# 512-column products in the output projections and in the dilated attention's q, k, v

## The chip, the cores and the metric

The kernel runs on one core of one Trainium2 chip. The metric is device time in microseconds (us) of one execution. Before the change the median of three runs is 1854.78 us (1853.63 to 1857.01).

## The reference

512 tokens of 1024 features go through two blocks, all in float32. Block 1 mixes sparse attention (8 heads) with a state-space scan, projects with `w_o`, and runs a gated feed-forward net with a short convolution. Block 2 has a gated convolution mixer and a dilated attention with three groups of windows and dilations. Cut to what the change touches:

```python
# block 1, feed-forward
u = causal_dwconv(h @ w_up, conv_w, conv_b);  a, v = split(u, 2)
x = x + gt2 * ((silu(a) * v) @ w_down)            # 2816 -> 1024
# block 2, convolution mixer
x = x + (b_gate * conv3(c_gate * u) * silu(z)) @ conv_w_out      # 2048 -> 1024
# block 2, dilated attention: 16 heads of 64, groups (128,1), (512,4), (2048,16)
proj = h @ w_in;  qkv, z = proj[..., :9216], proj[..., 9216:]
for g in range(3):
    q = rms_norm(qkv[:, :, g, 0], q_gain[g]);  k = rms_norm(qkv[:, :, g, 1], k_gain[g])
    o[g], lse[g] = dilated_group_attention(q, k, qkv[:, :, g, 2], bias[g], *DILATED_GROUPS[g])
alpha = softmax(stack(lse));  y = sum(alpha * stack(o)) * silu(z)
x = x + y @ attn_w_out                              # 1024 -> 1024
```

## The kernel before

**Products.** Each float32 product is made of three: high·high, high·low, low·high, where a number is split into a rounded high part and the rest. `wload` (L100) brings a weight piece of 128 x 1024 numbers by a DMA on SP's queue (L109) into `raw`; ACT rounds it into `whi` (all activations are recorded at L59), DVE, or POOL at a few places, subtracts to get `wlo` (L95). `raw`, `whi` and `wlo` have three buffers each. There are two loops of matmuls. `gemm_b` (L122, matmul at L133) holds the weights still and moves 512 tokens past them, so a matmul is 512 columns wide. `gemm_a` (L138, matmul at L146) holds 128 tokens still and moves weights: before, 256 columns of weights per matmul. Two tiles of 128 tokens then share one PSUM bank of 512 columns, so that a chunk of 256 weight columns for all 512 tokens takes two banks.

**Projections back to 1024 features** go through `proj_out` (L405): four chunks of 256 columns, two banks each, then `residual` (L376) adds to x and `square_sums` (L286) prepares the next norm. It serves `w_o`, `w_down` (two halves of 11 row blocks), `conv_w_out`, and `attn_w_out`, the latter once for heads 0 to 13 (seven pairs) and once for the last pair, where `done` (L1475) adds x and writes the output. PSUM has eight banks. `divide(4, 4, "acc", "acc")` (L430) gives the feed-forward and convolution stages four accumulation banks and four others; the attention has four accumulation banks (`acc`), three (`pst`) for transposes and scores, and one (`pso`) for the output of a pair.

**The attention** (`block2_attn`, L1227) walks over eight pairs of heads. For pair p:

- `v12`, the values of groups 1 and 2, is one `gemm_a` chunk of 256 columns; ACT copies it out of PSUM (`values_out`). For even p there also is `v0` and the gate `z` of two pairs, by `gemm_b`.
- For each group g a `gemm_a` chunk of 256 columns gives q and k in two banks. ACT squares the banks, DVE sums (L1333), a chain of small DVE operations makes the inverse root (`rsqrt`), and DVE multiplies the banks by it into `qn` (L1336) in SBUF, which has one buffer of 256 columns.
- PE transposes q (L1343) and k (L1351) of `qn` into `pst` banks; ACT and DVE split them into `qh`, `ql`, `kbh`, `kbl`.
- PE makes the scores (L1365 for group 0, L1382 for groups 1 and 2: twelve matmuls into two `pst` banks). DVE adds the bias and takes the extreme of each row (L1373, L1389), ACT takes exponentials into `P0`, `P1`, `P2`.
- When all three groups are there, the weights `wg` of the groups are worked out (L1405 to L1419); those of group 0 go through DRAM because its tokens lie in another order. DVE scales `P1` and `P2` block by block (L1435, 16 operations of 128 x 128), PE transposes them (L1436) and multiplies with `v12` (L1442); the same for group 0 (L1451, L1460, L1464). L1468 multiplies with the gate, and the result is split into `yh`, `yl`.

**Order.** Every engine runs its own instructions in one fixed order, which the Tile framework's scheduler decides from a simulated timeline and the priority of the code (program order, unless `tc.high_priority()` raises it). So work of the next chunk or the next pair is put between the steps of this one; where a tile has one buffer, the next writer waits for the last reader.

Of the kernel before, what the change touches and what calls it, by code (L numbers as in the profile page):

```python
# [10 lines left out]
F32 = mybir.dt.float32  # L11
# [8 lines left out]
D = 1024  # L20
# [31 lines left out]
def build(tc, A, out, dump=None, stop=None):  # L52
# [15 lines left out]
    with ExitStack() as top:  # L68
# [31 lines left out]
        def wload(ap, k, c, gain=None, eng=None, part=None, step=None):  # L100
# [4 lines left out]
            for k0 in range(0, k, step) if part is None else [part * step]:  # L105
# [3 lines left out]
                dma(raw[:, :n], ap[:, k0 * c:k0 * c + n])  # L109
# [141 lines left out]
        def ada(which):  # L251
# [4 lines left out]
            if not half:  # L256
                asum[which] = sml.tile([128, 256], F32, name="asum", bufs=3)
# [8 lines left out]
        def gate_rows(slot, tiles):  # L266

            for h, g in enumerate(tiles):
                pb = bank(acc)
                for k in range(4):  # L270
                    c = slot * 8 + h * 4 + k
                    d = sml.tile([128, 128], F32, name="gdiag")
# [13 lines left out]
        def square_sums(tiles, c, n):  # L286

            for t in range(tiles.start, tiles.stop):
                sq = sml.tile([128, 256], BF, name="nsq")
                act(sq, x[:, t, c * 256:(c + 1) * 256], AF.Square, accum_out=xss[:, n, t, c:c + 1])  # L290
# [3 lines left out]
        def scaled(g, twice=False):  # L294
# [4 lines left out]
            if not twice:  # L299
                ss = sml.tile([128, 2], F32, name="nss")  # L300
                V.tensor_reduce(ss, xss[:, 0, tl], axis=AX.X, op=OP.add)
                rs = mean_rsqrt(ss, [128, 2], "n", 1.0 / D)
            else:
# [3 lines left out]
                V.tensor_reduce(m, xss[:, 0, tl], axis=AX.X, op=OP.add)  # L307
                V.tensor_scalar(m, m, 1.0 / D, EPS, op0=OP.mult, op1=OP.add)
                V.tensor_reduce(s2, xss[:, 1, tl], axis=AX.X, op=OP.add)
# [66 lines left out]
        def residual(ps, tiles, c, gate, last, gain=None, rs=None):  # L376

            o = x[:, tiles, c * 256:(c + 1) * 256]
            src = ps.rearrange("p (t c) -> p t c", t=2)
            if gate is None:  # L380
                V.tensor_add(o, src, o)
            else:
                t = sml.tile([128, 2, 256], F32, name="rtmp", bufs=1)
                gc = gate[c // 2][:, c % 2 * 256:c % 2 * 256 + 256]
                if rs is None:
                    V.tensor_tensor(t, src, gc[:, None, :].to_broadcast([128, 2, 256]), op=OP.mult)
                else:
                    for q in range(2):
                        k = q if rs.shape[1] == 2 else tiles.start + q
                        V.scalar_tensor_tensor(t[:, q], src[:, q], rs[:, k:k + 1], gc, op0=OP.mult, op1=OP.mult)  # L390
                (V if c == 3 and last else P).tensor_tensor(o, o, t, op=OP.add)
            if last:
                square_sums(tiles, c, 0)
                if gain is not None:
                    V.tensor_tensor(o, o, gain[:, None, c * 256:(c + 1) * 256].to_broadcast([128, 2, 256]), op=OP.mult)
                    square_sums(tiles, c, 1)
# [8 lines left out]
        def proj_out(xh, xl, wname, k0, k, gate, gains=None, done=None, last=True, gain=None, rs=None, halves=(0, 1)):  # L405

            for c in range(4):
                pb = [bank(acc) if b in halves else None for b in range(2)]
                w = wload(A[wname][c][:, k0 * 256:(k0 + k) * 256], k, 256, None if gains is None else gains[:, k0:])
                tb = [t for b, t in enumerate(token_banks(pb, natural)) if b in halves]  # L410
                if c == 3 and last:
# [4 lines left out]
                for b in halves:  # L416
                    if done is not None:
                        done(pb[b], b, c)
                        continue
                    residual(pb[b], slice(2 * b, 2 * b + 2), c, gate, last, gain, rs)  # L420
                    if c == 3 and last and b == 0 and len(halves) == 2:
# [7 lines left out]
        divide(4, 4, "acc", "acc")  # L429
# [92 lines left out]
def block1_mix(tc, nc, E):  # L522
# [669 lines left out]
    def out_s():  # L1192
        gate_rows(4, gt1)
        ry = mean_rsqrt(ssq[:, 1], [128, 4], "o", 0.25 / 512)
        proj_out(xh[:, 4:8], xl[:, 4:8], "w_o", 4, 4, gt1, gains, rs=ry, last=False)

    def out_a(b):

        rs = mean_rsqrt(ssq[:, 0, 2 * b:2 * b + 2], [128, 2], "o2", 1.0 / 512)
        proj_out(xh, xl, "w_o", 0, 4, gt1, gains, rs=rs, halves=(b,))  # L1200
# [26 lines left out]
def block2_attn(tc, nc, E):  # L1227
# [16 lines left out]
    with ExitStack() as ph:  # L1244
# [20 lines left out]
        v0 = None  # L1265
        gz = [None] * 8
        for p in range(8):

            def gate_out(pz):
                for q in range(2):  # L1270
                    gz[p + q] = pp.tile([128, S], F32, name=f"yl{p + q}")
                    act(gz[p + q], pz[q], AF.Silu)
# [337 lines left out]
```

## Time and profile before

| what | value |
|---|---|
| median of three runs | 1854.78 us (1853.63 to 1857.01) |
| the profiled execution | 1851.47 us, its span 1849.1 us |
| PE busy | 97% of the span, 12252 matmuls |
| DVE busy | 59% |
| ACT busy | 43% |
| POOL busy | 16% |
| DMA | 189.55 MB, mean 103 GB/s |

The span runs from the first to the last instruction of the trace; 2.4 us of the profiled execution lie outside it. PE is TensorE, DVE VectorE, ACT ScalarE, POOL GpSimd, SP the engine that issues DMAs. Up to about 375 us runs the mixer of block 1, then the feed-forward net to about 750 us, the convolution mixer to about 1210 us, and the dilated attention to the end; two pairs of heads take 146.7 us there (the rows of one pair recur two pairs later by that much).

### The profile page before, as it was taken

The page shows a single profiled execution, that of the slowest core. Times are in us where ns is not written, and L with a number is a line of the kernel's source. Part 1 is how long each engine was busy: PE and PEld are TensorE (multiplying, and loading weights), DVE is VectorE, ACT ScalarE, POOL GpSimd, SP SyncE. Part 2 cuts the span into 40 slices and gives each one's busy share as a digit, 9 for nine tenths or more (in the row PEclk, how much of TensorE's full clock was granted, in tenths as well). Part 3 has the DMA queues.
Part 4 walks back from the last instruction along what each step waited for, and adds up shares of the span by engine and source line. Part 5 has one row for each costly group of instructions (what it writes and reads, how often), then busy time and mean ns, then how long its engine had stood idle before and what let it go on. Part 6 is the DMA issues. An engine that isn't in the chain of part 4 may idle for free.

```text
span 1849.1 us, 31264 instructions
## 1 busy us (share of the span) xinstructions
PE 1785.7 (97%) x12252; PEld 1580.2 (85%) x12252; DVE 1090.8 (59%) x2722; ACT 798.5 (43%) x1625; POOL 292.4 (16%) x238
## 2 busy tenths in 40 slices
PE   5998999999999999899999999999999999999998
PEld 3787657888898889888898888989989999989998
DVE  8796867965535554633333333346665665765775
ACT  3532666564413433432322323335455464554552
POOL 3665202431111111500000000120000000000000
PEclk9999999999999999999999999999999999999999
DMA  8358640423232233232332323222232222322222
GB/s 336 93 150 237 210 138 12 136 83 103 86 98 102 92 87 96 70 103 93 102 92 91 103 91 103 81 93 80 81 93 70 81 92 70 93 69 81 81 65 63
DMA packets 84660, 189.55 MB, mean 103 GB/s; under 512 B 31649, under 2 KB 39073, under 8 KB 84513
## 3 DMA queue, kind: packets, MB, share of 16 engines
q1 hardware_dynamic: 84512, 187.56, 31.9%
q8 instruction: 96, 1.57, 0.4%
q14 instruction: 52, 0.42, 0.1%
HBM read 182.74 MB, written 4.78 MB: 101 GB/s over the span
## 4 chain that ended last, share of the span: by engine, by line
PE 87%; DVE 7%; DMA 2%; issue 1%; ACT 1%; POOL 1%; SPq 0%; DVEq 0%; POOLq 0%; ACTq 0%
PE bank L133 38%; PE bank L146 36%; PE bank L1382 1%; PE bank L1138 1%; PE bank L1134 1%; PE bank L1365 1%; PE bank L1442 1%; PE bank L1115 1%; PE bank L1436 1%; PE bank L226 1%; DVE wlo L98 1%; PE bank L1460 1%; PE bank L1464 1%; PE bank L1351 1%; PE bank L344 1%
## 5 line engine op out<-in xcount | busy, mean ns | idle before, releaser
L95 DVE TENSOR_TENSOR wlo<-raw,whi 128x1024 fp32r<-128x1024 f32 (+3 forms) x245 | 304.9, 1245 | 313.0 <-ACT whi L59 309.3
L59 ACT ACTIVATE whi<-raw 128x1024 fp32r<-128x1024 f32 (+2 forms) x257 | 266.2, 1036 | 461.5 <-PE bank L133 252.7
L133 PE MATMUL bank<-xl,whi 128*128 128x512 f32 (+1 forms) x1120 | 290.4, 377 | 6.6 <-DVE xl L358 6.3
L133 PE MATMUL bank<-xh,whi 128*128 128x512 f32 (+1 forms) x1120 | 292.1, 379 | 2.1 <-ACT xh L59 2.1
L133 PE MATMUL bank<-xh,wlo 128*128 128x512 f32 (+1 forms) x1120 | 285.6, 376 | 0.0
L133 PEld LDWEIGHTS bank<-xl,whi 128*128 128x128 f32 x1120 | 203.6, 189 | 46.5 <-DVE xl L358 8.2
L133 PEld LDWEIGHTS bank<-xh,whi 128*128 128x128 f32 x1120 | 203.2, 191 | 42.3 <-ACT xh L59 4.0
L133 PEld LDWEIGHTS bank<-xh,wlo 128*128 128x128 f32 x1120 | 203.1, 189 | 37.7
L146 PE MATMUL bank<-whi,xh 128*128 128x256 f32 (+1 forms) x1312 | 200.8, 287 | 2.9 <-DVE rtmp L390 1.7
L146 PE MATMUL bank<-wlo,xh 128*128 128x256 f32 (+1 forms) x1312 | 197.3, 287 | 0.0
L146 PE MATMUL bank<-whi,xl 128*128 128x256 f32 (+1 forms) x1312 | 196.8, 286 | 0.0
L146 PEld LDWEIGHTS bank<-whi,xh 128*128 128x128 f32 x1312 | 175.4, 191 | 6.8 <-issue 2.6
L146 PEld LDWEIGHTS bank<-wlo,xh 128*128 128x128 f32 x1312 | 173.6, 191 | 2.6 <-issue 2.1
L146 PEld LDWEIGHTS bank<-whi,xl 128*128 128x128 f32 x1312 | 173.7, 191 | 1.4 <-issue 1.2
L59 ACT ACTIVATE P<-P,stat 128x128 f32<-128x128 f32 (+1 forms) x192 | 79.8, 417 | 55.5 <-DVE stat L1389 33.2
L59 ACT ACTIVATE ptt<-bank 128x512 f32<-128x512 f32 x112 | 61.5, 580 | 95.3 <-PE bank L1436 42.4
L201 DVE SCALAR_TENSOR_TENSOR cy<-bank,taps,cy 128x384 f32<-128x384 f32 (+3 forms) x176 | 72.9, 477 | 33.8 <-ACT cy L59 33.8
L146 PE MATMUL bank<-wlo,hh 128*128 128x256 f32 x608 | 86.0, 283 | 0.0
L146 PE MATMUL bank<-whi,hl 128*128 128x256 f32 x608 | 86.0, 283 | 0.0
L146 PE MATMUL bank<-whi,hh 128*128 128x256 f32 x608 | 86.0, 283 | 0.0
L512 POOL TENSOR_TENSOR cy<-cy,sz 128x512 f32<-128x512 f32 x16 | 28.7, 1793 | 354.9 <-ACT sz L59 354.9
L146 PEld LDWEIGHTS bank<-whi,hh 128*128 128x128 f32 x608 | 79.0, 192 | 0.3
(385 smaller groups left out, 2511.8 us busy)
## 6 DMA issues: line engine op xcount, KB each, us to landing
raw<-in_conv_w_in_dram SPq DMA_DIRECT2D x64, 512.0 KB, 3.4
adaw<-in_w_ada_dram SPq DMA_DIRECT2D x48, 512.0 KB, 5.0
raw<-in_w_qk_dram SPq DMA_DIRECT2D x48, 512.0 KB, 3.5
raw<-in_w_up_dram SPq DMA_DIRECT2D x44, 512.0 KB, 3.4
raw<-in_w_v_dram SPq DMA_DIRECT2D x24, 512.0 KB, 3.5
raw<-in_w_down_dram SPq DMA_DIRECT2D x16, 512.0 KB, 3.6
raw<-in_conv_w_out_dram SPq DMA_DIRECT2D x16, 512.0 KB, 3.9
raw<-in_w_o_dram SPq DMA_DIRECT2D x12, 512.0 KB, 4.2
```

The lines of the kernel that those rows point to most:

```text
L59: return nc.scalar.activation(o, i, fn, **kw)
L95: (eng or V).tensor_tensor(lo, src, f(hi), op=OP.subtract)
L98: V.scalar_tensor_tensor(lo, src, scale, f(hi), op0=OP.mult, op1=OP.subtract)
L133: mm(ps[:, tok], a[:, q, j * 128:(j + 1) * 128], b[:, k0 + q, tok], start=n == 0 and i == 0 and h != 1, stop=n == len(w) - 1 and i == 3 * ...
L146: mm(ps, a[:, base + k0 + q, tok], b[:, q, :], start=first and n == 0 and i == 0 and o == 0, stop=last and n == len(w) - 1 and i == 3 * kn ...
L201: V.scalar_tensor_tensor(o, i, t, o, op0=OP.mult, op1=OP.add)
L226: mm(pb[32 * q:32 * q + 32, :256], csil[:, r * 4 + q, 3 - i:35 - i], raw[:, q * 256:(q + 1) * 256], start=i == i0 and r == 0, stop=i > i0 ...
L344: nc.tensor.transpose(pt[:, (2 * a + q) * 128:(2 * a + q + 1) * 128], xn[q][:, k * 128:(k + 1) * 128], ident)
L512: P.tensor_tensor(y, y, sz, op=OP.mult)
L1115: mm(ps[:, :n], qs[:, h, qt], kk[:, br, kvh, 0:n], start=kk is ksh, stop=kk is ksl)
L1134: transpose(pt[:, s * 128:(s + 1) * 128], prs[hl][:, j * 128:(j + 1) * 128], ident)
L1138: mm(po[par * 64:par * 64 + 64, kvh * 256:(kvh + 1) * 256], vsw[:, j, br, kvh * 64:kvh * 64 + 64], ptt[:, par, :], start=False, stop=br == ...
```

## The change

- `proj_out` works in chunks of 512 weight columns for `w_down`, `conv_w_out` and `attn_w_out`: a matmul moves 512 columns, and a chunk takes four banks, one for each tile of 128 tokens. Where a norm follows (the last call for a residual), the second half is cut into two chunks of 256. `w_o` stays as it was (`wide=False`). The weights are packed in chunks of 512; the chunks of 256 are then read by DMAs with strides. The stages have all eight banks in `acc`.
- In the attention a pair has two chunks of 512 columns, `rows(0)` with v1, v2 and q, k of group 0, and `rows(1)` with q, k of groups 1 and 2; each takes all four `acc` banks. Each bank is copied out under a raised priority into `qn`, now 512 columns wide and with one buffer as before (v1, v2 by DVE, q and k of group 0 by ACT; for `rows(1)` ACT and DVE by turns). Squares, sums, inverse roots (two chains for a chunk, each for 256 tokens) and multiplications then work on SBUF.
- `v0` and `z` of the next two pairs are made after `rows(0)` of an odd pair (`values_0`, `gate_out`); pair 0 makes its own at the start, and `v12` of pair 0 no longer stands between its pieces.
- `P1` and `P2` are each scaled by one operation of 128 x 1024, by DVE for group 1 and by POOL for group 2.
- `done` writes 128 tokens x 512 columns. Some small tiles of the first stages move to another pool.

By count of matmuls 4824 of 256 columns are replaced by 2412 of 512: 684 in `w_down` and `conv_w_out`, 1536 in the attention, 192 in `attn_w_out`. DVE goes from 2724 to 2772 instructions, ACT from 1303 to 1337, POOL from 240 to 246, SP from 508 to 506.

```diff
                 raw = W["p"].tile([128, 1024], F32, name="raw")
-                dma(raw[:, :n], ap[:, k0 * c:k0 * c + n])
+                if len(ap.shape) == 3:
+                    dma(raw[:, :n].rearrange("p (k c) -> p k c", k=kn), ap[:, k0:k0 + kn, :])
+                else:
+                    dma(raw[:, :n], ap[:, k0 * c:k0 * c + n])
...
-            for c in range(4):
-                pb = [bank(acc) if b in halves else None for b in range(2)]
-                w = wload(A[wname][c][:, k0 * 256:(k0 + k) * 256], k, 256, None if gains is None else gains[:, k0:])
-                tb = [t for b, t in enumerate(token_banks(pb, natural)) if b in halves]
...
+            last_wide = wide and done is None and last
+            cols_ = [(0, 512), (512, 256), (768, 256)] if last_wide else [(0, 512), (512, 512)] if wide else \
+                [(c * 256, 256) for c in range(4)]
+            if last:
+                parts[0] = len(cols_)
+            for i, (c0, cw) in enumerate(cols_):
+                nt = 512 // cw
+                tiles = [slice(t, t + nt) for b in halves for t in range(2 * b, 2 * b + 2, nt)]
+                pb = [bank(acc) for t in tiles]
+                tb = [[(p_[:, q * cw:(q + 1) * cw], natural(t.start + q)) for q in range(nt)] for p_, t in zip(pb, tiles)]
+                if wide:
+                    ap = A[wname][c0 // 512].rearrange("p (k c) -> p k c", c=512)[:, k0:k0 + k, c0 % 512:c0 % 512 + cw]
+                else:
+                    ap = A[wname][i][:, k0 * 256:(k0 + k) * 256]
+                w = wload(ap, k, cw, None if gains is None else gains[:, k0:])
...
+                for p_, t in zip(pb, tiles):
                     if done is not None:
-                        done(pb[b], b, c)
+                        done(p_, t.start, c0)
...
-        divide(4, 4, "acc", "acc")
+        divide(8, "acc", "acc", "acc")
...
+        def values_0(p):
+
...
         for p in range(8):
-            def values_out(pbs, o):
-                for b, pb in enumerate(pbs):
-                    act(o[:, 2 * b:2 * b + 2, :], pb.rearrange("p (t c) -> p t c", t=2))
+            def rows(c):
+
+                pbs = [bank(acc) for _ in range(4)]
+                w = wload(A["w_pair"][2 * p + c], 8, 512)
+                gemm_a([[(pb, natural(t))] for t, pb in enumerate(pbs)], xh, xl, w)
+                o = at.tile([128, 4, 512], F32, name="qn")[:, :, :512 if c else 256]
+                n = 8 if c else 4
+                ss = at.tile([128, 4, 8], F32, name="qss", bufs=2)[:, :, :n]
+                for b in range(2):
+                    for t in (2 * b, 2 * b + 1):
+
+                        with tc.high_priority():
+                            if c == 0:
+                                V.tensor_copy(v12[:, t], pbs[t][:, 0:256])
+                            if c and t % 2:
+                                V.tensor_copy(o[:, t], pbs[t])
+                            else:
+                                act(o[:, t], pbs[t] if c else pbs[t][:, 256:512])
+                        sq = at.tile([128, 512], F32, name="sq")[:, :64 * n]
+                        act(sq, o[:, t], AF.Square)
+                        V.tensor_reduce(ss[:, t], sq.rearrange("p (a d) -> p a d", d=64), axis=AX.X, op=OP.add)
+                    rs = mean_rsqrt(ss[:, 2 * b:2 * b + 2], [128, 2, n], f"q{c}", 1.0 / 64)
+                    for t in range(2):
+                        v = o[:, 2 * b + t].rearrange("p (a d) -> p a d", d=64)
+                        TT(v, v, rs[:, t, :, None].to_broadcast([128, n, 64]), op=OP.mult)
+                return o
             if p == 0:
 
                 wz = wload(A["w_z"][0], 8, 256, eng=P)
-                w = wload(A["w_v12"][0], 8, 256, eng=P)
                 pz = [bank(acc), bank(acc)]
-                gemm_b(oz, xh, xl, wz, [(0, 0), (1, 0)])
-                gemm_a([tb[0]], xh, xl, w[:1], last=False)
-                gemm_b(oz, xh, xl, wz, [(0, 1), (1, 1)])
-                gemm_a([tb[1]], xh, xl, w[:1], last=False)
-                gemm_a(tb, xh, xl, w[1:], first=False)
-                gate_out(pz)
+                gemm_b([(pz[0], 0), (pz[1], 1)], xh, xl, wz, [(0, 0), (1, 0), (0, 1), (1, 1)])
+                gate_out(0, pz)
+                v0 = values_0(0)
...
-            if p > 0:
-                w = wload(A["w_v12"][p], 8, 256)
-                pbs = [bank(acc), bank(acc)]
-                gemm_a(token_banks(pbs, natural), xh, xl, w)
-                values_out(pbs, v12)
...
+            qn_ = [rows(0), None, None]
+            v0_ = v0
+            if p % 2 and p < 7:
+
+                v0_ = values_0(p + 1)
+                wz = wload(A["w_z"][(p + 1) // 2], 8, 256)
+                pz = [bank(acc), bank(acc)]
+                gemm_b([(pz[0], 0), (pz[1], 1)], xh, xl, wz)
+                gate_out(p + 1, pz)
             for g in range(3):
                 kb = (p * 3 + g) % 2
-                w = wload(A["w_qk"][p * 3 + g], 8, 256)
-                qn = at.tile([128, 4, 256], F32, name="qn", bufs=1)
-                ss = at.tile([128, 4, 4], F32, name="qss", bufs=2)
-                pbs = [bank(acc), bank(acc)]
-                gemm_a(token_banks(pbs, natural), xh, xl, w)
-                for b, pb in enumerate(pbs):
-                    sq = at.tile([128, 8, 64], F32, name="sq")
-                    act(sq, pb.rearrange("p (a d) -> p a d", d=64), AF.Square)
-                    V.tensor_reduce(ss[:, 2 * b:2 * b + 2, :].rearrange("p t a -> p (t a)"), sq, axis=AX.X, op=OP.add)
-                rs = mean_rsqrt(ss, [128, 4, 4], "q", 1.0 / 64)
-                for b in range(2):
-                    TT(qn[:, 2 * b:2 * b + 2].rearrange("p t (a d) -> p (t a) d", d=64),
-                       pbs[b].rearrange("p (a d) -> p a d", d=64),
-                       rs[:, 2 * b:2 * b + 2, :].rearrange("p t a -> p (t a)")[:, :, None].to_broadcast([128, 8, 64]),
-                       op=OP.mult)
+                if g == 1:
+                    both = rows(1)
+                    qn_[1:] = [both[:, :, 0:256], both[:, :, 256:512]]
+                qn = qn_[g]
 
...
             for g in (1, 2):
+                pw = P12[g].rearrange("p t h k -> p (t h) k")
+                (V if g == 1 else P).tensor_tensor(pw, pw, wg[:, g].rearrange("p t h -> p (t h)")[:, :, None].to_broadcast([128, 8, 128]), op=OP.mult)
                 for rr in range(2):
                     pt = bank(pst)
                     for r in range(2):
                         for h in range(2):
                             t = 2 * rr + r
                             pr_ = P12[g][:, t, h, :]
-                            TS(pr_, pr_, wg[:, g, t, h:h + 1], None, op0=OP.mult)
                             transpose(pt[:, (r * 2 + h) * 128:(r * 2 + h + 1) * 128], pr_, ident)
                     ptt = at.tile([128, 512], F32, name="ptt", bufs=3)
                     act(ptt, pt)
...
-        def done(pb, b, c):
-            tag, bufs = (("ptt", 3), ("qh", 2), ("ql", 2), ("ptt", 3), ("sq", 1), ("qh", 2), ("ql", 2), ("ptt", 3))[2 * c + b]
-            o = at.tile([128, 512], F32, name=tag, bufs=bufs).rearrange("p (t c) -> p t c", t=2)
-            TT(o, pb.rearrange("p (t c) -> p t c", t=2), x[:, 2 * b:2 * b + 2, c * 256:(c + 1) * 256], op=OP.add)
-            dma(out.rearrange("(p t) c -> p t c", p=128)[:, 2 * b:2 * b + 2, c * 256:(c + 1) * 256], o)
+        def done(pb, t, c0):
+            tag, bufs = (("ptt", 3), ("qh", 2), ("ql", 2), ("ptt", 3), ("sq", 1), ("qh", 2), ("ql", 2), ("ptt", 3))[c0 // 128 + t]
+            o = at.tile([128, 512], F32, name=tag, bufs=bufs)
+            TT(o, pb, x[:, t, c0:c0 + 512], op=OP.add)
+            dma(out.rearrange("(p t) c -> p t c", p=128)[:, t, c0:c0 + 512], o)
...
-    A["w_down"] = chunks(a["w_down"][0], 256)
+    A["w_down"] = chunks(a["w_down"][0], 512)
+    order = ((1, 2), (2, 2), (0, 0), (0, 1), (1, 0), (1, 1), (2, 0), (2, 1))
+    A["w_pair"] = chunks(np.stack([qkv[:, g, i] for g, i in order], 2).reshape(D, -1), 512)```

The lines of the kernel move by the edit: `gemm_a`'s matmul is L149 after it, the transposes of q and k L1367 and L1375, the scores of groups 1 and 2 L1406, the transposes of `P1` and `P2` L1461.

PE, around the scores of group 1 of pair 3 (L1382, two banks) and the transposes of group 2 (L1343, L1351). Before:

```order
L1382 MATMUL bank_14587<-kbl0_11343,qh_14559 128x256
L1382 MATMUL bank_14587<-kbh0_11341,ql_14560 128x256
L133 MATMUL bank_14939<-xl_11237,whi_14934 128x512
L1343 MATMUL bank_14736<-ident_75,qn_14614 128x128 [waits DVE_49,PE_49]
L133 MATMUL bank_14939<-xl_11237,whi_14934 128x512
L133 MATMUL bank_14939<-xh_11236,wlo_14935 128x512 x4
L133 MATMUL bank_15017<-xh_11236,whi_15007 128x512 x4
```

After, the same place (`bank_13890` is the first bank of `rows(1)` of pair 4):

```order
L1406 MATMUL bank_13464<-kbl0_10631,qh_13436 128x256
L1406 MATMUL bank_13464<-kbh0_10629,ql_13437 128x256
L1367 MATMUL bank_13479<-ident_75,qn_13381 128x128 [waits PE_49]
L1367 MATMUL bank_13479<-ident_75,qn_13381 128x128 x3
L1375 MATMUL bank_13488<-ident_75,qn_13381 128x128 [waits DVE_49,PE_49]
L1375 MATMUL bank_13488<-ident_75,qn_13381 128x128 x3
L149 MATMUL bank_13890<-whi_13896,xh_10524 128x512 [waits Activation_49]
```

Before, value products of the next pair stand behind the scores, between and behind the transposes. After, the transposes follow the scores at once, and the next product waits for ACT.

ACT, the same place, after the change (`bank_13479` holds the transposed q of group 2, `bank_13662` to `bank_13664` are the banks of `rows(0)` of pair 4, `qn_13786` their place in SBUF, the one buffer that `qn_13381` had):

```order
L59 ACTIVATE P1_12878,stat_12880<-P1_12878,stat_12880 128x128 [waits DVE_49] x4
L59 ACTIVATE qh_13484<-bank_13479,qkg_10626 128x512 [waits PE_49]
L59 ACTIVATE qn_13786<-bank_13662 128x256 [waits PE_49]
L59 ACTIVATE qn_13786<-bank_13663 128x256
L59 ACTIVATE qn_13786<-bank_13665 128x256
L59 ACTIVATE qn_13786<-bank_13664 128x256
L59 ACTIVATE kbh1_10630<-bank_13488,qkg_10626 64x4x128
```

The copies are new; they stand behind four exponentials and the split of q.

PE, the last scores of pair 7 (groups 2). Before:

```order
L1382 MATMUL bank_18295<-kbl1_11344,qh_18267 128x256
L1382 MATMUL bank_18295<-kbh1_11342,ql_18268 128x256
L146 MATMUL bank_18552<-whi_18561,yh_11235 128x256 x4
L146 MATMUL bank_18552<-wlo_18562,yh_11235 128x256 x6
```

After:

```order
L1406 MATMUL bank_16189<-kbl1_10632,qh_16161 128x256
L1406 MATMUL bank_16189<-kbh1_10630,ql_16162 128x256
L1461 MATMUL bank_16239<-ident_75,P1_15700 128x128 [waits DVE_49,PE_49]
L1461 MATMUL bank_16239<-ident_75,P1_15700 128x128 x3
L1461 MATMUL bank_16250<-ident_75,P1_15700 128x128 [waits PE_49]
```

Before, 184 matmuls of `attn_w_out` stand between the last score and the end of the pair's own work; after, all of them stand ahead of the last scores, and the transposes of `P1` come next.

## Rows read from the trace of the kernel before

**Rows 1.** The page, part 1: busy time of each engine, share of the span, instructions.

```profile
PE 1785.7 (97%) x12252; PEld 1580.2 (85%) x12252; DVE 1090.8 (59%) x2722; ACT 798.5 (43%) x1625; POOL 292.4 (16%) x238
```

**Rows 2.** Windows: stretch, us, busy PE, PEld, DVE, ACT, POOL, PE clock, DMA share, GB/s.

```profile
1400.00:1500.00 100.00, 100.00 (x809) 95.96 (x808) 70.23 (x222) 51.93 (x119) 3.34 (x3) 1.00 0.26 80
1600.00:1700.00 100.00, 100.00 (x766) 91.52 (x765) 64.06 (x208) 53.08 (x122) 5.94 (x3) 1.00 0.25 80
```

**Rows 3.** Timeline, PE, `w_down`: start, us, engine, line, operation, count.

```profile
700.53 1.12 PE L146 MATMUL bank<-wlo,hh 128*128 128x256 f32 x8
701.49 1.12 PE L146 MATMUL bank<-whi,hl 128*128 128x256 f32 x8
```

**Rows 4.** Timeline, PE, `w_up`: twelve matmuls from the first start to the second.

```profile
420.89 1.07 PE L133 MATMUL bank<-xh,wlo 128*128 128x512 f32 x4
...
423.61 0.62 PE L133 MATMUL bank<-xh,wlo 128*128 128x512 f32 x2
```

**Rows 5.** Timeline, PE, scores of group 1 in one pair, and what follows.

```profile
1435.17 0.28 PE L1382 MATMUL bank<-kbl,qh 128*128 128x256 f32 x1
...
1435.64 0.28 PE L1382 MATMUL bank<-kbh,ql 128*128 128x256 f32 x1
...
1436.36 0.39 PE L146 MATMUL bank<-whi,xh 128*128 128x256 f32 x2
```

**Rows 6.** Timeline, DVE, the same scores.

```profile
1435.96 0.29 DVE L1389 CUSTOM_DVE_ANT_0 P<-bank,bias 128x128 f32<-128x128 f32 x1 [0.43 <-PE bank L1382]
...
1436.17 0.29 DVE L1389 CUSTOM_DVE_ANT_0 P<-bank,bias 128x128 f32<-128x128 f32 x1
```

**Rows 7.** Timeline, ACT, the same scores: first and last of eight exponentials.

```profile
1436.29 0.40 ACT L59 ACTIVATE P<-P,stat 128x128 f32<-128x128 f32 x1 [2.94 <-DVE stat L1389]
...
1439.01 0.39 ACT L59 ACTIVATE P<-P,stat 128x128 f32<-128x128 f32 x1
```

**Rows 8.** Groups by line and form: busy us, mean ns, idle before.

```profile
L95 DVE TENSOR_TENSOR wlo<-raw,whi 128x1024 fp32r<-128x1024 f32 x226 | 280.9, 1243 | 307.0 <-ACT whi L59 304.1 <-POOL cy L466 1.9
...
L95 POOL TENSOR_TENSOR wlo<-raw,whi 128x1024 fp32r<-128x1024 f32 x12 | 28.9, 2419 | 67.9 <-ACT whi L59 67.4 <-DVE rs_ym L168 0.5
...
L59 ACT ACTIVATE nsq<-x 128x256 bf16<-128x256 f32 x64 | 26.0, 407 | 41.2 <-DVE x L381 12.4 <-POOL x L391 11.3 <-DVE x L395 9.3
...
L59 ACT ACTIVATE qh<-bank,qkg 128x512 fp32r<-128x512 f32 x24 | 16.4, 685 | 7.5 <-PE bank L1343 7.0
...
L59 ACT ACTIVATE v<-bank 128x512 f32<-128x512 f32 x24 | 14.3, 600 | 21.7 <-PE bank L146 16.1 <-PE bank L1305 5.6
```

**Rows 9.** Chain of waits, transposes of P0: start, us, work.

```profile
1387.27 0.87 PE bank L1460 x8
```

**Rows 10.** Timeline, PE, the end: last score of pair 7.

```profile
1808.21 0.28 PE L1382 MATMUL bank<-kbh,ql 128*128 128x256 f32 x1
```

**Rows 11.** Timeline, DVE and ACT, the end: group weights, scaling, gate, output.

```profile
1813.58 0.16 DVE L1414 TENSOR_TENSOR den<-wg,m0p 128x8 f32<-128x8 f32 x1
...
1814.49 0.32 DVE L1419 TENSOR_TENSOR wg<-wg,den 128x8 f32<-128x8 f32 x3
1814.77 3.23 DVE L1435 TENSOR_SCALAR P<-P,wg 128x128 f32<-128x128 f32 x16
...
1819.42 1.80 DVE L1451 TENSOR_SCALAR P<-P,w 128x128 f32<-128x128 f32 x7
...
1833.86 0.69 DVE L1468 TENSOR_TENSOR ptt<-bank,yl 128x512 f32<-128x512 f32 x1 [11.09 <-PE bank L1464]
...
1834.59 0.63 ACT L59 ACTIVATE yh<-ptt 128x512 fp32r<-128x512 f32 x1
...
1844.18 0.69 DVE L1479 TENSOR_TENSOR ptt<-bank,x 128x512 f32<-128x512 f32 x1
```

**Rows 12.** Timeline, PE, after the longest wait, at the norm after `w_down`.

```profile
754.00 3.64 PE L344 MATMUL bank<-ident,adaw 128*128 128x128 f32 x16 [6.75 <-DVE adaw L317]
```

**Rows 13.** Windows, PE alone, around that wait.

```profile
740.00:760.00 20.00, 12.80 (x93) 0.83 0.25 81
```

More of the change, by code (lines that the diff above doesn't have):

```diff
@@ L374, in norm_t, with residual @@
                         P.tensor_scalar(t, t, rfs[g][:, q:q + 1], None, op0=OP.mult)
-        def residual(ps, tiles, c, gate, last, gain=None, rs=None):
-            o = x[:, tiles, c * 256:(c + 1) * 256]
-            src = ps.rearrange("p (t c) -> p t c", t=2)
+        def residual(ps, tiles, c0, cw, i, gate, last, gain=None, rs=None):
+            o = x[:, tiles, c0:c0 + cw]
+            nt = tiles.stop - tiles.start
+            src = ps.rearrange("p (t c) -> p t c", t=nt)
             if gate is None:
@@ L403, in token_banks, with proj_out @@
                     for b, pb in enumerate(banks)]
[L405 to L411 removed]
+        def proj_out(xh, xl, wname, k0, k, gate, gains=None, done=None, last=True, gain=None, rs=None, halves=(0, 1),
+                     wide=True):
+            last_wide = wide and done is None and last
[13 more added lines that the diff above has]
+                w = wload(ap, k, cw, None if gains is None else gains[:, k0:])
+                if c0 + cw == D and last and not done:
                     for t in tb:
@@ L415, in proj_out @@
                     gemm_a(tb, xh, xl, w)
-                for b in halves:
+                for p_, t in zip(pb, tiles):
                     if done is not None:
-                        done(pb[b], b, c)
+                        done(p_, t.start, c0)
                         continue
-                    residual(pb[b], slice(2 * b, 2 * b + 2), c, gate, last, gain, rs)
-                    if c == 3 and last and b == 0 and len(halves) == 2:
+                    residual(p_, t, c0, cw, i, gate, last, gain, rs)
+                    if c0 + cw == D and last and t.start == 0 and len(halves) == 2:
                         ahead.append((scaled(0, gain is not None), gain is not None))
@@ L1263, in block2_attn, with gate_out @@
         wd = dr.tile([512, 2], F32, name="wd")
[L1265 removed]
         gz = [None] * 8
[L1267 to L1276 removed]
+        def gate_out(p, pz):
+            for q in range(2):
+                gz[p + q] = pp.tile([128, S], F32, name=f"yl{p + q}")
+                act(gz[p + q], pz[q], AF.Silu)
@@ new lines, in values_0 @@
+        def values_0(p):
+            w = wload(A["w_v0"][p // 2], 8, 256)
+            pbs = [bank(acc), bank(acc)]
+            gemm_b([(pbs[0], 0), (pbs[1], 1)], xh, xl, w)
+            v0 = at.tile([128, 4, 256], F32, name="v0", bufs=2)
+            for q, pb in enumerate(pbs):
+                vt = at.tile([128, S], F32, name="vt")
+                act(irm(vt), rim(pb))
+                pt = bank(pst)
+                for i in range(4):
+                    transpose(pt[:, i * 128:(i + 1) * 128], vt[:, i * 128:(i + 1) * 128], ident)
+                act(v0[:, :, q * 128:q * 128 + 128], pt.rearrange("p (i c) -> p i c", i=4))
+            return v0
```

66 lines of the change are left out of this document (23 added, 43 removed).

## The prediction

> **What bounds the kernel now.** I read the busy shares first: PE is busy 97% of the span, no other engine more than 59% [rows 1]. The share is an average, so the windows come next: in the attention PE is busy for the whole of both stretches shown, at the full granted clock, while DVE is at 64 to 70% and ACT at 52 to 53% [rows 2]. So PE's own work sets the time: work taken from PE counts in full until something else is late, and a wait given to PE counts in full too. The timeline then gives the price of a matmul as the distance from start to start, since each one's duration overlaps the next. 256 columns: eight in 0.96 us, 120 ns each [rows 3]. 512 columns: twelve in 2.72 us, 226.7 ns each [rows 4].
>
> **What the change removes.** Two matmuls of 256 columns (240 ns) become one of 512 (226.7 ns): 13.3 ns less. With 2412 of the new ones that is 32.2 us: 684 in `w_down` and `conv_w_out` (9.1), 1536 in the attention (20.5, or 2.6 a pair), 192 in `attn_w_out` (2.6). The rows at 512 columns are of `gemm_b`, where the weights stand still; the new ones have tokens standing still and the same 128 x 128 to load, so I take their price. From below, the saving could be nothing if the loads got in the way, but the 256-column rows of the same loop hide a load behind only 120 ns, and 512 columns leave twice that.
>
> The Trainium skill ("TensorE: Matmul & The Clock Gate", section "Wait — 56ns, not 53.3ns?") has a matmul start N columns / 2.4 GHz plus about 2.5 ns after the one before. By it two of 256 and one of 512 would differ by 2.5 ns, and the 2412 would save 6.0 us. The trace disagrees on both widths (120 and 226.7 ns where the page gives 109 and 216), and its two rows are the ones I use.
>
> **What it adds: wait A, on the copy into `qn`.** Until now `qn` was written from PSUM late, after the square sums, with value products on PE meanwhile. Now `qn` holds groups 1 and 2 and has one buffer, so the banks of the next pair's `rows(0)` can only be copied out after the transposes of group 2; PE's next product waits for that copy, with nothing between. This occurs after each pair but the last, seven times. I set T at the first of the twelve scores of group 1.
> - PE: twelve scores at 0.12 us end their issue at T+1.44 (ten took 1.19 [rows 5]). Four transposes of q at 0.109 [rows 9] end at T+1.88. Those of k need the first score bank read by DVE: its last score starts at T+0.72, DVE starts 0.32 later ([rows 5, 6]: 1435.64 to 1435.96) and takes four steps 0.21 apart [rows 6], which is T+1.9 and with the release about T+2.05; k ends at T+2.5.
> - ACT: the exponentials start 0.33 after DVE ([rows 6, 7]), T+1.37, and go 0.39 apart [rows 7]; four stand ahead, to T+2.93. Then the split of q, 0.69, and the first copy, 0.41 as ACT's operation of 128 x 256 [rows 8]: T+4.03.
> - PE could go on at T+2.5 and does at T+4.05: 1.55, and 0.15 before it for k. So 1.7 us each, **12 us** for seven. Bounds: 0.9 if the split and the copy take only what lies between the starts of neighbouring ACT instructions or the exponentials run ahead, 2.6 if two more instructions of 0.4 to 0.6 get in ahead; 6 to 18 us.
>
> **Wait B**, the same after group 0: where `rows(0)` of the next pair or values follow the transposes of group 0 at once, PE waits for a copy of a `rows(1)` bank, behind the split of q (0.69) and at 0.60 for 128 x 512 [rows 8]. The transposes of k cover half of that: 0.7 us, four times by the order, **2.8 us** (1.2 to 5.2).
>
> **The end, the largest single piece.** Before, 184 matmuls (22.1 us at 0.12) stand between the last score at 1808.21 [rows 10] and the end at 1849.1, 40.9 us in all, and cover the softmax of the last pair. Now they stand ahead of the last scores, and only the last pair's chain is left. Let V be the first of the last twelve scores: scores to V+1.44, the eight exponentials from V+1.35 to V+4.45 [rows 7], 0.2 for the exponential of the group weights, 1.25 for the weights ([rows 11]: 1813.58 to 1814.81), `P1` in one operation of 128 x 1024, 1.24 like `wlo` [rows 8], so the first transposes come at V+7.2 and PE idles 5.8 us. `P2` on POOL (2.42 [rows 8]) is there at V+8.4. Group 0's weights go through DRAM: 4.6 us from 1814.81 to 1819.42 [rows 11], V+10.6; most of the scalings, V+12.25; transposes, copies and products about 3.3, V+15.6; gate and split 0.69 + 0.63 [rows 11] and releases, V+17.2; 24 products at 227 ns, V+22.6; the last sum 0.32 after the last start and 0.69 long, V+23.6; then, as now, 4.2 us from the end of that sum (1844.87 [rows 11]) to the end of the span: V+27.8, or 26.5 from the last score. With the 22.1 us that were moved ahead, less the 40.9 of before: 7.7 us. After its longest idle time in this kernel, 6.75 us, PE took 3.64 us for 16 transposes [rows 12] instead of 16 x 0.109 = 1.7, and the granted clock of the stretch was 0.83 [rows 13], a mean of the two levels, 1.2 and 2.4 GHz. An idle time of 5.8 us should do much the same: 1.6. Together **9.3 us**, with 5 (no clock loss, chain shortened) to 13 as bounds.
>
> **The start.** 24 half-width products of `v12` (24 x 0.12 = 2.9 us) no longer fill the wait for the norm of pair 0, where `z` alone is left ahead of `v0`: **1.5 us**, between 0 and 2.9.
>
> **The rest, at nothing.** The 16 scalings (3.23 us [rows 11]) become one on DVE and one on POOL: 2.0 us of DVE less a pair. Against that come four copies of `v12` (about 0.41 each), two of 128 x 512 (0.6 to 0.7) and one more chain of eleven small operations at 0.16 [rows 11]: 4.8 more. The net 3 us a pair lies in DVE's idle third [rows 2]; without that cover see the second rival. ACT's copies take the place of those of `v`. POOL is idle in the attention (3 to 6 us in 100 [rows 2]). The strided DMAs replace as many others behind three buffers, at a DMA share of 0.25 [rows 2].
>
> **Sum:** -32.2 + 12 + 2.8 + 9.3 + 1.5 = -6.6 us. That makes 1844.9 for the profiled execution; it lies 3.3 us under the median (1851.47 against 1854.78), so the median goes to **1848.2**. The bounds of the four costs (12 to 39 together) cannot all fall on one side; for this case alone I take 1841 to 1855.
>
> **Rivals.**
> 1. *The copies come in time* (chance 0.17): DVE and ACT finish the scores and exponentials before PE has done its products, or the release of a bank is seen later than it is needed, so A and B vanish. For: ACT is idle half of the time. Against: the order puts four exponentials and a split ahead of the copy. Time: -32.2 + 9.3 + 1.5 = -21.4, 1833.4.
> 2. *DVE becomes the bound in the four pairs without `v0` and `z`* (0.20), slower than before. `v0` and `z` are 96 products of 512 columns, 21.8 us, of the 146.7 us of two pairs; so a pair without them leaves PE 62.4, now some 60 us, and DVE has about 47 (67% of 146.7, less 5 for four `wlo`, halved), now 50. That is 83%, and DVE's work comes in bunches: sums, two chains and multiplications after each chunk, all on the way to the transposes, with the `wlo` of the next chunk queued between. If it is late by three `wlo` (3 x 1.24 = 3.7 us [rows 8]) in each, 15 us come on top: -6.6 + 15 = +8.4, 1863.2. It decides once all waits together pass 32.2 us. Against: now DVE has a third of its time free.
> 3. *The fixed part of a matmul does not halve* (0.02): with tokens standing still, 512 columns take 237.5 ns, 2.5 less than two of 256; then 6.0 instead of 32.2 us are saved, +19.6, 1874.4. The page of the Trainium skill named above gives this figure. Against: both widths in the rows show the same 13.3 ns above the columns themselves.
>
> **How the numbers follow.** The forecast has 0.61. The range of 1834 to 1864 takes it whole, and about half of each of the first two rivals; the third and the other halves are left out, 0.2 in all. About 0.2% (3.7 us) is what a measurement of this kernel can tell from no change, so "same" is 1851.1 to 1858.5. The forecast's case lies under that for two thirds (0.41), in it for a third; with the first rival that makes 0.59 faster, 0.22 same (with a part of the second), 0.19 slower.
>
> **What would show it.** Right: `w_down` and `conv_w_out` 9 us shorter, products of L149 226 to 228 ns apart, PE idle about 1.7 us before L149 after the transposes of L1375 seven times, ACT named as releaser; about 6 us of idle PE before the first L1461 of the last pair. Wrong: no waits on ACT before L149 (rival 1); waits of L1367 or L1375 on DVE, or of L149 on `wlo`, of some us in odd places of a pair (rival 2); 237 ns (rival 3).

## The result and the profile after

The changed kernel takes 1867.88 us (median of four runs, 1864.71 to 1870.53) against 1854.2 us of the kernel before (median of four); the ratio is 1.008, 95% interval [1.006, 1.010]. It is slower by 13.7 us, where 6.6 us less had been forecast; the time lies outside the range. The profiled execution has a span of 1864.4 us.

The page of the kernel after, part 1 (compare [rows 1]), and two windows of its attention (compare [rows 2]):

```profile
PE 1770.2 (95%) x9840; PEld 1456.5 (78%) x9840; DVE 1084.5 (58%) x2770; ACT 813.6 (44%) x1647; POOL 313.3 (17%) x244
```

```profile
1400.00:1500.00 100.00, 98.28 (x543) 79.52 (x542) 63.58 (x231) 54.83 (x138) 10.82 (x5) 1.00 0.28 79
...
1600.00:1700.00 100.00, 97.20 (x510) 80.04 (x509) 62.76 (x201) 56.08 (x133) 5.63 (x3) 1.00 0.30 85
```

PE has less to do (1785.7 to 1770.2 us) and waits more; DVE is not busier than before (1090.8 and 1084.5 us). The timeline of `w_down` gives twelve matmuls of 512 columns in 2.72 us, 226.7 ns each, the forecast price:

```profile
690.21 0.62 PE L149 MATMUL bank<-wlo,hh 128*128 128x512 f32 x2
...
692.93 0.62 PE L149 MATMUL bank<-wlo,hh 128*128 128x512 f32 x2
```

Where the 15.3 us of span went is read from the first transposes of the three norms. They stand at 368.3, 754.0 and 1203.0 us before and at 370.0, 754.3 and 1209.5 after. So the stage ahead of them is 1.7 us longer, the feed-forward net 1.4 us shorter, the convolution mixer 6.2 us longer, the attention 8.8 us longer. The waits of PE from 400 to 1240 us, of the kernel after (engine, line waited for: us in all, times, longest):

```profile
PE bank L349 <- DVE adaw L322: 12.5, 2, 6.8
PE bank L349 <- DVE x L388: 4.2, 1, 4.2
PE bank L136 <- ACT xh L59: 0.5, 1, 0.5
```

Before, the transposes waited 8.9 us there. The timeline of PE after shows the new part: the first half's 16 transposes, and then not products, but four of the second half's transposes, which wait for DVE; the products stand behind them:

```profile
754.26 3.65 PE L349 MATMUL bank<-ident,adaw 128*128 128x128 f32 x16 [6.84 <-DVE adaw L322]
763.60 1.09 PE L349 MATMUL bank<-ident,adaw 128*128 128x128 f32 x4 [5.69 <-DVE adaw L322]
764.34 1.20 PE L136 MATMUL bank<-xh,whi 128*128 128x256 f32 x4
```

Before, the first products followed those 16 transposes [rows 12] at 757.33. The same happens at the start of the feed-forward net, where the longest wait before was 3.5 us:

```profile
379.46 1.11 PE L349 MATMUL bank<-ident,adaw 128*128 128x128 f32 x4 [7.57 <-DVE adaw L322]
```

The waits of PE from 1240 us to the end, after; before there was none:

```profile
PE bank L149 <- ACT qn L59: 6.5, 8, 1.3
PE bank L1461 <- DVE P L1454: 5.8, 1, 5.8
PE bank L136 <- ACT qn L59: 3.9, 3, 1.3
PE bank L149 <- ACT yh L59: 1.5, 1, 1.5
```

The two lines on `qn` are the waits A and B (eleven, 10.4 us); those on `P` and `yh` belong to the end.

### The profile page after: what moved, and what is told of

Its sections match the earlier page's. It is cut to its first block, busy times and chain, and to the rows that moved or that the text cites. A ratio compares the mean times of both kernels' runs of the same rounds, so it can differ in the third digit from the quotient of the medians.

```text
span 1864.4 us, 26449 instructions
## 1 busy us (share of the span) xinstructions
PE 1770.2 (95%) x9840; PEld 1456.5 (78%) x9840; DVE 1084.5 (58%) x2770; ACT 813.6 (44%) x1647; POOL 313.3 (17%) x244
## 4 chain that ended last, share of the span: by engine, by line
PE 85%; DVE 7%; DMA 3%; ACT 2%; issue 2%; POOL 1%; SPq 0%; DVEq 0%; ACTq 0%; POOLq 0%
PE bank L136 37%; PE bank L149 35%; DMA adaw<-in_w_ada_dram 2%; PE bank L1389 1%; PE bank L1158 1%; PE bank L1467 1%; PE bank L1154 1%; PE bank L1406 1%; PE bank L229 1%; PE bank L1461 1%; PE bank L1485 1%; ACT P L59 1%; PE bank L1135 1%; PE bank L1489 1%; DMA adaw<-in_w_c_dram 1%
## 5 line engine op out<-in xcount | busy, mean ns | idle before, releaser
L59 ACT ACTIVATE whi<-raw 128x1024 fp32r<-128x1024 f32 (+3 forms) x255 | 266.0, 1043 | 501.0 <-PE bank L136 260.5
L95 DVE TENSOR_TENSOR wlo<-raw,whi 128x1024 fp32r<-128x1024 f32 (+3 forms) x245 | 301.4, 1230 | 302.4 <-ACT whi L59 301.4
L136 PE MATMUL bank<-xl,whi 128*128 128x512 f32 (+1 forms) x1120 | 290.4, 378 | 7.1 <-DVE xl L363 6.8
L136 PE MATMUL bank<-xh,whi 128*128 128x512 f32 (+1 forms) x1120 | 289.8, 379 | 4.6 <-ACT qn L59 3.9
L136 PE MATMUL bank<-xh,wlo 128*128 128x512 f32 (+1 forms) x1120 | 286.7, 376 | 0.0
L136 PEld LDWEIGHTS bank<-xl,whi 128*128 128x128 f32 x1120 | 204.0, 190 | 47.1 <-DVE xl L363 8.7
L136 PEld LDWEIGHTS bank<-xh,whi 128*128 128x128 f32 x1120 | 202.8, 190 | 45.1 <-ACT qn L59 4.7
L136 PEld LDWEIGHTS bank<-xh,wlo 128*128 128x128 f32 x1120 | 203.8, 190 | 37.5
L149 PE MATMUL bank<-whi,xh 128*128 128x512 f32 (+2 forms) x800 | 207.8, 359 | 9.0 <-ACT qn L59 6.2
L149 PE MATMUL bank<-whi,xl 128*128 128x512 f32 (+2 forms) x800 | 207.5, 356 | 0.0
L149 PE MATMUL bank<-wlo,xh 128*128 128x512 f32 (+2 forms) x800 | 206.1, 354 | 0.0
L149 PEld LDWEIGHTS bank<-whi,xh 128*128 128x128 f32 x800 | 134.6, 191 | 32.0 <-ACT qn L59 7.9
L149 PEld LDWEIGHTS bank<-whi,xl 128*128 128x128 f32 x800 | 135.2, 189 | 22.0 <-issue 2.0
L149 PEld LDWEIGHTS bank<-wlo,xh 128*128 128x128 f32 x800 | 134.7, 189 | 20.8 <-issue 1.2
L59 ACT ACTIVATE ptt<-bank 128x512 f32<-128x512 f32 x104 | 57.7, 578 | 87.8 <-PE bank L1461 35.8
L149 PE MATMUL bank<-wlo,hh 128*128 128x512 f32 (+1 forms) x380 | 92.7, 347 | 0.0
L149 PE MATMUL bank<-whi,hl 128*128 128x512 f32 (+1 forms) x380 | 92.7, 347 | 0.0
L149 PE MATMUL bank<-whi,hh 128*128 128x512 f32 (+1 forms) x380 | 92.6, 347 | 0.0
L59 ACT ACTIVATE P<-P,stat 128x128 f32<-128x128 f32 (+1 forms) x192 | 80.0, 420 | 22.1 <-DVE stat L1397 12.0
L149 PEld LDWEIGHTS bank<-whi,hh 128*128 128x128 f32 x380 | 62.6, 189 | 9.0
```

Source lines behind the costliest of these rows:

```text
L59: return nc.scalar.activation(o, i, fn, **kw)
L95: (eng or V).tensor_tensor(lo, src, f(hi), op=OP.subtract)
L136: mm(ps[:, tok], a[:, q, j * 128:(j + 1) * 128], b[:, k0 + q, tok], start=n == 0 and i == 0 and h != 1, stop=n == len(w) - 1 and i == 3 * ...
L149: mm(ps, a[:, base + k0 + q, tok], b[:, q, :], start=first and n == 0 and i == 0 and o == 0, stop=last and n == len(w) - 1 and i == 3 * kn ...
```

## The experiments

Ratios are to the kernel before, run on the same chip.

**1. The split of PSUM.** The forecast had no term for `divide(8, "acc", "acc", "acc")`. Two kernels tell its cost. In the changed kernel, the split of before:

```diff
-        divide(8, "acc", "acc", "acc")
+        divide(4, 4, "acc", "acc")
```

> Only the split of PSUM in the feed-forward and convolution stages goes back to four accumulation banks and four for the norm's transposes. Theory 'one pool of eight': the long waits of PE at the three norms (1.8 + 7.6 us, 5.7 us, 4.2 us after the change; 0.4 + 3.5, 0.5, and 2.2 + 1.7 before) come from transposes and products taking banks out of one ring, so they go back to the values of before and some time at the half clock goes too: about 12 us less than the change, near 1855 us; no new wait between chunks, since a chunk's first bank is long read when the next needs it. Rival 'new tiling of the residual' (sums and squares over 128 tokens x 512 columns come later): the waits stay, 1866 to 1869 us.

Measured: 1857.91 us, 1.0032 [1.0014, 1.0051]. From 400 to 1240 us PE waits 9.8 us for the transposes' input, near the 8.9 of before, and the wait of 7.6 us at the start of the feed-forward net is gone; one of 3.3 us is left there, as before (from 367 to 400 us PE waits 3.9 us before, 9.9 in the change, 3.7 here):

```profile
PE bank L349 <- DVE adaw L322: 9.8, 3, 6.8
PE bank L136 <- ACT xh L59: 1.1, 1, 1.1
```

And the opposite edit, alone, in the kernel before:

> The kernel before with one pool of eight banks in these stages and nothing else changed. 'One pool of eight': the waits at the norms appear here too, 10 to 14 us over the kernel before, 1864 to 1868 us. 'New tiling of the residual': no change, 1853 to 1856 us.

Measured: 1865.75 us, 1.0085 [1.0062, 1.0109], with narrow products throughout. Its waits from 400 to 1240 us are those of the change:

```profile
PE bank L344 <- DVE adaw L317: 12.5, 2, 6.8
PE bank L344 <- DVE x L381: 4.2, 1, 4.2
PE bank L133 <- ACT xh L59: 1.0, 1, 1.0
```

So the pool of eight costs 14.8 us in the kernel before and 7 to 10 in the change (10.0 us between the two medians, 8.9 by the ratios, 6.7 when each median is taken against the kernel before beside it), with narrow products as with wide ones. The stages from the first norm to the second and from there to the third show it: 2.7 and 10.8 us longer with the one pool than in the kernel before, 2.0 and 8.6 in the change than in the run with four banks. The waits are not all of it: the granted clock from 740 to 780 us, a mean of its two levels, is 0.91 before and 0.79 with the one pool. With two pools, the first products of a stage have banks of their own and are ordered between the two halves of the norm; with one, the scheduler puts transposes of the second half ahead of them, and the products wait with those. That the wait of 4.2 us at the attention's norm comes from banks that `conv_w_out`'s last chunk still holds when the new pools are laid over the old ones fits the releaser (L388, the sum that reads them), but was not tried by itself.

**2. The projections alone.** `w_down` and `conv_w_out` wide, four banks and four, the small tiles of the first stages as in the change, the attention as before.

> 512-column products in w_down and conv_w_out alone, with four banks for them and four for the norms' transposes; the attention and attn_w_out as before. Theory 'the projections gain what their matmuls save, the attention loses': 684 products x 13.3 ns = 9.1 us, of which the feed-forward and convolution stages of the run with four banks showed 3.4 + 2.4 = 5.8; so 6 to 9 us faster than the kernel before, 0.3 to 0.5%. Rival 'the wide chunks lose at the norms even with four banks' (the last bank of a chunk is summed later): no gain, within 2 us of the kernel before.

Measured: 1847.07 us, 0.9963 [0.9950, 0.9976], 5.9 us faster by the medians and 6.9 by the ratio; ahead of the kernel before and of the change. In its profile the stages from the first norm to the third are 3.4 and 2.5 us shorter. With `attn_w_out` wide too:

> As the run with the projections alone, and attn_w_out in 512 columns too; q, k, v of the attention as before. Theory 'the end of the attention needs narrow pieces of attn_w_out as filling': four banks for a chunk instead of two leave less to put between the last pair's steps, so the 2.6 us that its matmuls save are used up by a wait at the end, 0 to 6 us slower than the run with the projections alone. Rival 'the end is lost by the two wide chunks of q, k, v': 2 to 3 us faster than that run.

Measured: 1846.56 us, 0.9968 [0.9957, 0.9980]. No difference from the run above, so the rival's 2 to 3 us did not come. The theory is not excluded at its lower end: PE now waits 1.5 us for `yh` and 0.5 us for `ptt` in the attention, where the run above has no wait, against 2.6 us that the matmuls were to save.

**3. The attention alone.** As the change, with four banks and `w_down`, `conv_w_out` narrow.

> The attention of the change (wide q, k, v and attn_w_out) with narrow w_down and conv_w_out and four banks there. Theory 'the attention loses by itself': its products save 27 us, waits take 18 (10.4 at the copies into qn, 7.3 at the end), slower transposes and transitions 18, so 8 to 13 us slower than the kernel before. Rival 'the attention is even and the loss is only that of the PSUM pool': within 3 us of the kernel before.

Measured: 1866.13 us, 1.0066 [1.0050, 1.0082], 13.2 us slower. Its waits in the attention are those of the change within 0.6 us. So the attention loses by itself. The two halves add up: 13.2 - 5.9 = 7.3, and the run with both and four banks lies 7.0 over the kernel before.

**4. The waits at the copies.** In the change, `qn` is made once:

```diff
+        qn_all = at.tile([128, 4, 512], F32, name="qn")
...
-                o = at.tile([128, 4, 512], F32, name="qn")[:, :, :512 if c else 256]
+                o = qn_all[:, :, :512 if c else 256]
```

> The change, with qn as one tile made once and not anew for each chunk, so that the copies of the next pair's first chunk wait only for the transposes of group 1, whose half of the tile they write. Theory 'waits A and B on the copies': the seven waits of 1.3 us after the transposes of group 2 go, and with them their 0.2 us of slow transposes: 8 to 11 us less than the change, 1857 to 1860 us; the waits of 0.3 us after group 0 may stay. Rival 'DVE is the bound behind them': the time comes back as waits of transposes on DVE, within 3 us of the change.

Measured: 1880.62 us, 1.0166 [1.0133, 1.0199]: the waits on `qn` are gone, and the kernel is 12.7 us slower than the change by the medians, 16 by the ratios. From 1240 us on PE now waits for the scaled `P1` and `P0`:

```profile
PE bank L1462 <- DVE P L1455: 17.6, 5, 7.2
PE bank L1486 <- DVE P L1477: 3.0, 5, 1.1
```

The rival was right in kind and too low in size. The scheduler, free of the copy, moved the transposes of `P1` up to where DVE has not scaled it:

```profile
1427.50 0.61 PE L149 MATMUL bank<-whi,xl 128*128 128x512 f32 x2
1429.46 1.06 PE L1462 MATMUL bank<-ident,P 128*128 128x128 f32 x8 [1.34 <-DVE P L1455]
```

Then scaling by blocks, as the kernel before has it, in the change:

> The change with P1 and P2 scaled block by block on DVE again (16 operations of 128 x 128 a pair). Theory 'transposes in runs': a transpose that stands alone between products costs PE less (about 80 ns of start-to-start) than one in a run of four (110 to 130 ns), because its weights load behind the product; with block scaling the 128 transposes of P1 and P2 stand apart again, 4 us less, and at the end the first of them can start after one block, 1 us less of the idle 5.8 us: 1861 to 1864 us. Rival 'DVE has no time to spare': 2 us more DVE work in each pair delays it, 1868 to 1876 us.

Measured: 1868.51 us, 1.0099 [1.0076, 1.0122], no gain. The idle time at the end fell from 5.8 to 4.8 us as expected, but the transposes of `P1` and `P2` did not go apart: before, 80 of the 128 stand alone and the others in twos; in the change there are fifteen runs of four, seven of eight and one of twelve, and in this run mostly runs of four and of twelve. The time lies in the rival's range, but no new wait of PE for DVE came with it. The theory's price was wrong too. Before, a lone transpose and a product of 256 columns recur every 0.23 us, and the product alone takes 0.12, so that the transpose costs 0.11 and not 0.08:

```profile
1462.81 0.27 PE L1436 MATMUL bank<-ident,P 128*128 128x128 f32 x1
1462.83 0.37 PE L146 MATMUL bank<-wlo,xh 128*128 128x256 f32 x1
1463.04 0.27 PE L1436 MATMUL bank<-ident,P 128*128 128x128 f32 x1
```

In the change, eight in a run take 0.78 us and the product behind them 0.32 instead of 0.23, which makes 0.11 each as well:

```profile
1484.62 1.03 PE L1461 MATMUL bank<-ident,P 128*128 128x128 f32 x8
1485.40 0.48 PE L136 MATMUL bank<-xl,whi 128*128 128x512 f32 x1
1485.72 0.86 PE L136 MATMUL bank<-xh,wlo 128*128 128x512 f32 x3
```

Both edits with four banks:

> The change with four banks, qn as one tile and block scaling of P1 and P2. With the one tile alone the waits at the copies went but PE then waited 18 us for the scaled P1. Theory 'what PE waits for there is the one long scaling operation after the group weights': with blocks of 128 x 128 the first transpose is released 1 us earlier in each pair, and the waits fall from 18 to about 9 us: 1846 to 1856 us. Rival 'the order that the scheduler now chooses puts these transposes too early, whatever their scaling': the waits stay, 1862 to 1872 us.

Measured: 1858.67 us, 1.0024 [1.0013, 1.0036], the same as with four banks alone and between the two theories' ranges. The waits on the scaled `P1` are 15.5 us, 11.4 of them in the last two pairs; the other pairs have 0.8 us at most in one wait.

**5. The end.** The change with four banks, and in the last pair groups 1 and 2 as two chunks of 256 columns (copied out and normalized as in `rows`):

```diff
-                if g == 1:
+                if p == 7 and g:
+                    qn_[g] = rows_one(g - 1)
+                elif g == 1:
                     both = rows(1)
```

> The change with four banks (1857.9 us) and, in the last pair alone, groups 1 and 2 as two chunks of 256 columns again. Theory 'the end is lost because the last pair's groups come together': products of group 2 and of attn_w_out are then left to stand behind the last scores (by the order some 28 matmuls of 512 columns, 6.4 us), the idle 5.8 us before the first transpose of P1 goes and with it most of the half clock behind it, at a price of 1.3 us for 192 matmuls of 256 columns: 4 to 7 us less, 1851 to 1854 us. Rival 'the chain of the softmax ends the kernel whatever is put there': PE waits elsewhere before the end, within 2 us of 1857.9.

Measured: 1851.15 us, 0.9994 [0.9975, 1.0013]: 6.8 us less than with four banks alone, as the theory had it, and even with the kernel before. After the last scores there are products again, and the first transpose of `P1` follows them without idle time:

```profile
1828.67 0.39 PE L149 MATMUL bank<-whi,yl 128*128 128x512 f32 x1
1828.90 1.36 PE L1484 MATMUL bank<-ident,P 128*128 128x128 f32 x11
```

In the change, at the same place (timeline of PE; the last score and the first transpose):

```profile
1835.63 0.28 PE L1406 MATMUL bank<-kbh,ql 128*128 128x256 f32 x1
1841.69 2.79 PE L1461 MATMUL bank<-ident,P 128*128 128x128 f32 x12 [5.78 <-DVE P L1454]
```

## Why the prediction was wrong, point by point

- **The step that failed: "The rest, at nothing".** The new split of PSUM stood in the diff and in no term. It has no instruction of its own, and its price lies in the order around the norms: 7 to 10 us of the 20.3 between the forecast change (-6.6) and the measured one (+13.7). Neither of the two likely rivals had it. It did not decide the sign by itself: with four banks the kernel is still 7.0 us slower than before. The other half lies in the attention. There the forecast's terms add up to +2.5 us (-20.5, -2.6, 12, 2.8, 9.3, 1.5); its stage is 8.8 us longer in the trace, and the attention alone cost 13.2 by the medians. The waits were smaller than forecast and the end within 0.6 us of it, as the points below show, so here too it is the rest that had been put at nothing.
- **The saving by a matmul** was right: 226.7 ns measured in `w_down`. The projections alone gave 5.9 of the 9.1 us expected; the run's interval, 0.24 to 0.50%, reaches from 4.4 to 9.3 us and takes the 9.1 in. The trace of the change disagrees once more with the 2.5 ns above the columns that the Trainium skill gives for a matmul ("TensorE: Matmul & The Clock Gate", section "Wait — 56ns, not 53.3ns?"); by an estimate from that figure the 684 products would have saved 1.7 us, which lies below the interval.
- **Wait A** was right in place and chain, and somewhat large. PE resumes at T+4.06 in this pair, where T+4.05 was worked out:

```profile
1458.30 0.40 PE L1406 MATMUL bank<-kbh,qh 128*128 128x256 f32 x2
...
1462.36 1.19 PE L136 MATMUL bank<-xh,whi 128*128 128x512 f32 x4 [1.31 <-ACT qn L59]
```

  ACT's part of the same pair shows what the copy stood behind:

```profile
1461.34 0.69 ACT L59 ACTIVATE qh<-bank,qkg 128x512 fp32r<-128x512 f32 x1
1461.93 1.20 ACT L59 ACTIVATE qn<-bank 128x256 f32<-128x256 f32 x4
```

  The wait itself is 1.31 us and not 1.55, since the transposes of k end later; wait B is 0.32 and not 0.7. In all 10.4 us instead of 14.8. That these waits are worth their length is not shown: the run without them had another order and was slower.
- **The end** was right: 5.8 us idle before `P1` as worked out, and 28.7 us from the last score to the end of the span (26.5 and 1.6 for the clock had been forecast). The twelve transposes behind the idle time took 2.79 us, and the granted clock from 1842 to 1846 us was 0.50, the lower level. 6.8 us of the 9.3 were won back when the last pair kept its narrow chunks. That 6.75 us was the longest idle time of the kernel before is a slip: PE waits up to 11.2 us for a DMA in the first stage. No term rests on it.
- **The start** cost nothing that can be seen: at the norm of pair 0 (1195 to 1240 us) PE waits 3.9 us before and 4.2 with four banks, where 1.5 more had been put.
- **A term missing in the attention.** I summed the distances from each PE instruction's start to the next one's over four pairs (1419.6 to 1712.9 us before, 1440.5 to 1734.2 after): 293.2 and 293.7 us. The products of L149 take 12.6 us less (10.2 expected), the waits 6.2 us more, and everything else, transposes, scores and products with `P`, 6.9 us more for the same instructions. Nearly all of that, 6.7 us, stands with the 232 transposes (20.9 and 27.6 us). Some of it is only the place where it is counted, since a product behind a lone transpose starts soon and then takes longer itself; so the 2.4 us by which the products came out better belong against it. That leaves 4.5 us, some 1.1 us a pair that the forecast did not have, or 9 us for eight pairs if all are alike. The order of the transposes is what differs to the eye, but no run tried it by itself (the run with block scaling did not spread them), and a lone one costs no less than one in a run; the cause is open.
- **Rival 2** gave the time best (1863.2) for a reason that did not come: DVE is at 58% and no transpose of q or k waits for it.

## What to carry to other kernels

A change of the PSUM split can cost more than the edit it was made for is to save (14.8 us by itself here, against 6.6): look at what the scheduler places between the halves of a norm, and time the split alone. Take a saving of PE's own work where it brings no new waits (the projections here, 0.4%), and keep narrow pieces for the last unit of work, where they fill PE during the last chain. A price of one instruction read from its start to the next one's start can hide in the neighbour: compare the period of both. An edit that removes a wait in a scheduled kernel can give the scheduler another order, which has to be read again.

## What the hardware showed that was not expected

The same matmuls ran at different granted clocks. Up to the first norm the change, the run with the narrow last pair and the run with block scaling have the same 2508 matmuls in the same order. The windows of PE from 140 to 175 us (stretch, us, busy and count, granted clock, DMA share, GB/s) with the narrow last pair, in the change, and with block scaling:

```profile
140.00:175.00 35.00, 30.86 (x257) 1.00 0.87 236
```

```profile
140.00:175.00 35.00, 33.22 (x255) 0.90 0.83 231
```

```profile
140.00:175.00 35.00, 30.54 (x202) 0.80 0.74 198
```

The first norm's transposes stand at 367.8, 370.0 and 377.8 us there, with a mean granted clock of 0.97, 0.96 and 0.95 up to then. So spans of single profiles differ by up to 10 us ahead of anything in which these runs differ, and small effects are better read from a stage's own length or from medians. How much of the 10 us is the clock is not shown: the run with one `qn` tile and block scaling has 0.96 and stands at 368.2. A clock of 0.80 is a mean of the two levels, 1.2 and 2.4 GHz. Also, the last 38 products of `attn_w_out` before `P1` in the run with the narrow last pair stood 232 ns apart instead of 226.7 (1820.08 to 1828.67 us, 37 steps), at a granted clock of 1.00; in the change those from 1831.76 to 1834.09 us stand 233 ns apart. I have no cause for it.
